# Where the tiles lie in SBUF: large tiles at multiples of 2 KB, small ones behind them

## The chip, the cores and the metric

The kernel runs on one core of a Trainium2 chip. The metric is the device time of one execution, in microseconds; each execution on the chip gives one time, and before and after are compared by the median of several.

## The reference

Two layers (`DEPTH = 2`) of a transformer block over 256 tokens of width 1024, all in float32. Per layer:

```
h = rmsnorm(x);  proj = h @ w_in                 # 1024 x 8004
aq, ak, av, bq, bk, bv, cq, ck, cv, iq, ik, iw, gl = split(proj)
y_a = differential attention(aq, ak, av)         # 4 heads, two softmaxes each
y_b = stick-breaking attention(bq, bk, bv)       # 8 heads
y_c = top-64 sparse attention(cq, ck, cv), keys picked by iq, ik, iw
merged = sum over a, b, c of sigmoid(gl) * (y @ w_br)
x = x + merged @ w_out
x = x + relu(rmsnorm(x) @ w_up)^2 @ w_down       # 1024 -> 4096 -> 1024
x = x + sigmoid(rmsnorm(x) @ w_ple_gate) * (p @ w_ple_proj)
```

## The kernel before, in words

**The products.** Every large product is made of three matmuls on numbers split in two: an operand `a` is kept as a rounded part `ah` (type float32r) and the rest `al`, and `mm3` (line 387) adds `ah*bh + ah*bl + al*bh` into one bank of PSUM. Weights come by `load_unit` (line 370): SyncE (the queue SP) starts a DMA of 256 rows x 512 columns into a tile `w`, ScalarE rounds it into `wh`, VectorE (GpSimd for a few) writes the rest to `wl`. There are 4 tiles `w`, 6 `wh` and 6 `wl`, of 4 KB in each partition.

**Two shapes.** In `chunk_T` (line 416, through `T_steps`) the weights are stationary, 128 x 128 at a time, and the activations move through the array, 256 columns, one per token. It serves `w_up`, `w_down`, `w_out`, the branch products, the gates, `bq` and `bk`, and the first layer's last products. In `chunk` (line 392) it is the other way round: the activations are stationary and 512 columns of `wh` or `wl` move (324 for the index columns, 256 where the last chunk is cut in two). It serves `q`, `k` and `v`, and the second layer's last products. The trace names the moving operand first: `mmp<-xh,wh` has `xh` moving, and `mmp<-wh,xh` has `wh` moving. Results of most products go to `mmp`, those of `w_down` to `acc`.

**The activations.** `xh` and `xl` (8 KB each, class `Norm`, line 457) hold the normalised stream that `w_in`, `w_up` and `w_ple_gate` read. For `w_ple_gate` alone they are taken from the four general slots `g8` (`spare=True`), which otherwise hold heads and gates. `yh` and `yl` (4 KB, three of each, `acts4`, line 321) hold the attention's results, the merged branches, and in the MLP the 512 hidden columns of one chunk. So in the MLP, TensorE takes turns: 96 matmuls of `up` on `xh`, `xl`, then 96 of `down` on `yh`, `yl`.

**The order of the work.** All operations are first collected by `Program`, then put in order by a list scheduler with its own costs and due times (`schedule`, line 216), and emitted at line 290, which is therefore the line of all instructions in the trace. The scheduler sees slots by pool and tag, and how many are free; it knows nothing of addresses.

**The places.** A pool takes its room in the order in which pools are opened, and its slots follow one another, each rounded up to 32 bytes. The first free byte of a partition is 16,512, which is 8 x 2048 + 128. `cp` comes first, with the identity and all constants, the residual stream `xT` among them (together 15,808 bytes); then `wp` with `w`, `wh`, `wl`; then `sp` with everything else in the order of its first use. In the program of before this gives:

```
tile                          bytes into 2048   bytes into 256
w, wh, wl, working tiles t2        1600              64
xh, xl                             1600              64
g8 (heads, gates, spare xh, xl)    1216             192
working tiles big                  1216             192
xT                                 1952             160
v (av, bv, cv)                     1024               0
yh, yl                              256               0
```

A step along the inner part of a tile (one k-tile of activations is 1024 bytes, 128 columns of weights are 512 bytes) changes the middle column and not the last.

Of the kernel before, what the change touches and what calls it, by code (L numbers as in the profile page):

```python
# [293 lines left out]
def hybrid_block(ctx: ExitStack, tc: tile.TileContext, I, out):  # L294
    nc = tc.nc
    prog = Program(nc)
    V, S, G, T, Q = (prog.engine(e) for e in ("DVE", "ACT", "POOL", "PE", "SP"))

    cp = ctx.enter_context(tc.tile_pool(name="cp", bufs=1))
    wp = ctx.enter_context(tc.tile_pool(name="wp", bufs=6))  # L300
    sp = ctx.enter_context(tc.tile_pool(name="sp", bufs=2))
    pmm = ctx.enter_context(tc.tile_pool(name="pmm", bufs=2, space=PSUM))
    ptr = ctx.enter_context(tc.tile_pool(name="ptr", bufs=2, space=PSUM))
    psc = ctx.enter_context(tc.tile_pool(name="psc", bufs=2, space=PSUM))

    def const(name, shape, dt=F32):
        return prog.tile(cp, shape, dt, name)

    def t2k(name, cols=512):
        return prog.tile(sp, [P, cols], F32, name, tag="t2", bufs=T2, ahead=AHEAD_T2)  # L310
# [2 lines left out]
        return prog.tile(sp, shape, dt, name, tag="big", bufs=5, ahead=AHEAD_BIG)  # L313

    def small(name, shape, bufs, dt=F32, tag=None):
        return prog.tile(sp, shape, dt, name, tag=tag or name, bufs=bufs)

    def g8(name, dt=F32):
        return prog.tile(sp, [P, 8, SEQ], dt, name, tag="g8", bufs=4)
# [30 lines left out]
    prog.fixed = -LEAD_LOAD + X_AFTER  # L350
    load_x(1)
    pos_i = const("pos_i", [P, NB], I32)
    Q.dma_start(out=pos_i, in_=I["positions"].rearrange("o (b p) -> p (o b)", p=P), allow_slow_non_contiguous=True)

    GAINS = ("", "idx_k_norm", "a_k_norm", "c_k_norm", "a_q_norm", "c_q_norm")
    gains = const("gains", [P, len(GAINS), DEPTH, HD])
    for i, n in enumerate(GAINS):
        if n:
# [65 lines left out]
    def rsqrt_mean(ss, n, width):  # L424

        ms = small("ms", [P, 8], 4)
        V.tensor_scalar(ms[:, :n], ss, 1.0 / width, EPS, op0=OP.mult, op1=OP.add)
        r = small("rsq", [P, 8], 10)
        G.tensor_tensor(out=r[:, :n], in0=ms[:, :n], in1=half[:, :n], op=OP.pow)
        return r[:, :n]  # L430
# [26 lines left out]
    class Norm(Acts):  # L457
# [3 lines left out]
        def __init__(self, gains, spare=False):  # L461
            if spare:
                super().__init__([(g8("xh", FR), g8("xl", FR))])
            else:
                super().__init__([tuple(small(n, [P, 8, SEQ], 1, FR) for n in ("xh", "xl"))])
            self.gains = gains
            self.ss, self.made_row = None, None
# [77 lines left out]

    first_table = S.preload_act_table_set("trig_and_small")
    ncol0, ncol = const("ncol0", [P, 8]), const("ncol", [P, 50])

    def columns(src, dst):
# [32 lines left out]
    inv = const("inv", [P, 32])  # L582
# [29 lines left out]
    identb = const("identb", [P, P], BF)  # L612
    mA = const("mA", [P, NB, NB * P], BF)
    mB = const("mB", [P, P], BF)
    negone_r, ntri_r = const("negone_r", [P, P], FR), const("ntri_r", [P, P], FR)
# [487 lines left out]
```

## Time and profile before

| | us |
|---|---|
| median of 3 runs | 998.3 (998.06 to 998.92) |
| profiled execution | 996.65 |
| its span | 994.9 |
| TensorE busy | 975.9 (98%) |
| VectorE busy | 654.1 (66%) |
| ScalarE busy | 540.6 (54%) |

A busy share says how much of the span an engine had an instruction in it. Matmuls overlap one another, so the duration of one (some 280 ns for 256 columns) is longer than the step from its start to the start of the next; the step is what a stream of them costs.

### The profile page before, as it was taken

Reading aid. Unit: us, or ns where it says so; the run is one execution under the profiler, and the core shown is the slowest. Engines: PE = TensorE matmul, PEld = TensorE weight load, DVE = VectorE, ACT = ScalarE, POOL = GpSimd, SP = SyncE. Lnnn points to the kernel's source line nnn. Section 1 sums busy time; section 2 is a strip of 40 time slices with the busy share of each in tenths; the row PEclk is TensorE's granted clock in tenths of the full one; section 3 lists DMA queues with packets and bytes.
Section 4 is the critical chain, followed back from the end, with each engine's and each line's share of the span. In section 5 each row is a group of like instructions: output and inputs, shape, how many; then the busy total and the mean of one; then the engine's idle time right before and its main releaser. Section 6 shows DMA issues by size and latency. Waiting matters only on the chain.

```text
span 994.9 us, 18435 instructions
## 1 busy us (share of the span) xinstructions
PE 975.9 (98%) x7492; PEld 922.8 (93%) x7492; DVE 654.1 (66%) x1007; ACT 540.6 (54%) x768; POOL 155.7 (16%) x137
## 2 busy tenths in 40 slices
PE   7899999999999999999999999999999999999998
PEld 6888889989999999999989888898899999999997
DVE  7748997663767455557676599975557755555573
ACT  6537674465456444456573575645745545554462
POOL 1202122314220000000312112230152100000010
PEclk9999999999999999999999999999999999999999
DMA  7564255535565656556555543556265665566551
GB/s 262 177 208 134 83 159 170 175 119 173 192 176 187 197 183 193 189 170 197 155 168 170 190 132 110 151 169 191 85 192 171 194 206 171 174 194 202 194 171 43
DMA packets 89162, 168.59 MB, mean 169 GB/s; under 512 B 5690, under 2 KB 9204, under 8 KB 89076
## 3 DMA queue, kind: packets, MB, share of 16 engines
q1 hardware_dynamic: 89076, 167.40, 53.6%
q8 instruction: 59, 0.97, 0.4%
q14 instruction: 27, 0.22, 0.1%
HBM read 166.33 MB, written 1.05 MB: 168 GB/s over the span
## 4 chain that ended last, share of the span: by engine, by line
PE 94%; DVE 3%; ACT 1%; issue 1%; DMA 1%; SPq 0%; POOL 0%; ACTq 0%; DVEq 0%
PE mmp L290 68%; PE acc L290 18%; PE z L290 2%; PE sc L290 2%; PE oc L290 1%; DVE qo L290 1%; DVE wl L290 1%; PE qps L290 1%; PE ob L290 1%; ACT wh L290 1%; PE pps L290 1%; DMA xin<-in_x 1%; DVE io L290 1%; PE xps L290 0%; DVE rm L290 0%
## 5 line engine op out<-in xcount | busy, mean ns | idle before, releaser
L290 ACT ACTIVATE wh<-w 128x1024 fp32r<-128x1024 f32 (+1 forms) x316 | 330.5, 1050 | 216.7 <-PE mmp L290 106.2
L290 DVE TENSOR_TENSOR wl<-w,wh 128x1024 fp32r<-128x1024 f32 (+1 forms) x282 | 341.8, 1220 | 154.4 <-ACT wh L290 149.1
L290 PE MATMUL mmp<-xh,wh 128*128 128x256 f32 x1088 | 310.9, 286 | 3.5 <-DVE rm L290 3.5
L290 PE MATMUL mmp<-xh,wl 128*128 128x256 f32 x1088 | 310.4, 285 | 0.0
L290 PE MATMUL mmp<-xl,wh 128*128 128x256 f32 x1088 | 309.2, 284 | 0.0
L290 PEld LDWEIGHTS mmp<-xh,wh 128*128 128x128 f32 x1088 | 208.8, 192 | 5.7 <-ACT wh L290 4.2
L290 PEld LDWEIGHTS mmp<-xh,wl 128*128 128x128 f32 x1088 | 208.6, 192 | 1.2 <-issue 1.0
L290 PEld LDWEIGHTS mmp<-xl,wh 128*128 128x128 f32 x1088 | 208.6, 192 | 0.4
L290 PE MATMUL acc<-yh,wh 128*128 128x256 f32 x512 | 141.7, 277 | 0.0
L290 PE MATMUL acc<-yl,wh 128*128 128x256 f32 x512 | 141.4, 276 | 0.0
L290 PE MATMUL acc<-yh,wl 128*128 128x256 f32 x512 | 141.4, 276 | 0.0
L290 POOL TENSOR_TENSOR wl<-w,wh 128x1024 fp32r<-128x1024 f32 x34 | 84.0, 2472 | 224.6 <-ACT wh L290 224.6
L290 PE MATMUL mmp<-wh,xh 128*128 128x512 f32 (+2 forms) x296 | 113.3, 384 | 0.3 <-ACT av L290 0.3
L290 PE MATMUL mmp<-wh,xl 128*128 128x512 f32 (+2 forms) x296 | 112.5, 381 | 0.0
L290 PE MATMUL mmp<-wl,xh 128*128 128x512 f32 (+2 forms) x296 | 111.8, 379 | 0.2 <-DVE wl L290 0.2
L290 PEld LDWEIGHTS acc<-yh,wh 128*128 128x128 f32 x512 | 96.2, 188 | 0.0
L290 PEld LDWEIGHTS acc<-yl,wh 128*128 128x128 f32 x512 | 96.2, 188 | 0.0
L290 PEld LDWEIGHTS acc<-yh,wl 128*128 128x128 f32 x512 | 96.1, 188 | 0.0
L290 PE MATMUL mmp<-yl,wh 128*128 128x256 f32 x336 | 93.1, 278 | 0.2
L290 PE MATMUL mmp<-yh,wh 128*128 128x256 f32 x336 | 93.0, 277 | 0.2 <-ACT pp L290 0.2
L290 PE MATMUL mmp<-yh,wl 128*128 128x256 f32 x336 | 92.7, 277 | 0.0
L290 POOL TENSOR_TENSOR rsq<-ms,half 128x8 f32<-128x8 f32 (+3 forms) x30 | 47.9, 1602 | 215.2 <-DVE ms L290 215.2
(194 smaller groups left out, 1198.6 us busy)
## 6 DMA issues: line engine op xcount, KB each, us to landing
w<-in_w_in SPq DMA_DIRECT2D x120, 512.0 KB, 4.0
w<-in_w_up SPq DMA_DIRECT2D x64, 512.0 KB, 3.7
w<-in_w_down SPq DMA_DIRECT2D x64, 512.0 KB, 4.7
w<-in_w_out SPq DMA_DIRECT2D x16, 512.0 KB, 4.0
w<-in_w_ple_gate SPq DMA_DIRECT2D x16, 512.0 KB, 3.8
w<-in_w_br_a SPq DMA_DIRECT2D x8, 512.0 KB, 3.7
w<-in_w_br_c SPq DMA_DIRECT2D x8, 512.0 KB, 3.7
w<-in_w_br_b SPq DMA_DIRECT2D x8, 512.0 KB, 4.2
```

The costliest lines, as they stand in the source:

```text
L290: getattr(self.engines[op.eng], op.name)(*op.args, **op.kw)
```

## The change

A third and a fourth SBUF pool (`mp`, `lp`) are opened behind `sp`, and a tile goes to a pool by its size: a multiple of 2048 bytes to `sp`, else a multiple of 256 to `mp`, else to `lp`. Of the constants only `identb`, `negone_r`, `ntri_r` and `inv` (and `ident`, which is allocated directly) stay in `cp`. Tags, numbers of slots and operations stay.

```diff
+    mp = ctx.enter_context(tc.tile_pool(name="mp", bufs=1))
+    lp = ctx.enter_context(tc.tile_pool(name="lp", bufs=1))
...
+    def pool_for(shape, dt):
+        size = math.prod(shape[1:]) * mybir.dt.size(dt)
+        return sp if size % 2048 == 0 else mp if size % 256 == 0 else lp
+
     def const(name, shape, dt=F32):
-        return prog.tile(cp, shape, dt, name)
+        first = ("identb", "negone_r", "ntri_r", "inv")
+        return prog.tile(cp if name in first else pool_for(shape, dt), shape, dt, name)
...
     def small(name, shape, bufs, dt=F32, tag=None):
-        return prog.tile(sp, shape, dt, name, tag=tag or name, bufs=bufs)
+        return prog.tile(pool_for(shape, dt), shape, dt, name, tag=tag or name, bufs=bufs)
```

## Rows read from the trace of the kernel before

**Rows 1.** The page: busy time of the engines, and the chain by engine.
```profile
PE 975.9 (98%) x7492; PEld 922.8 (93%) x7492; DVE 654.1 (66%) x1007; ACT 540.6 (54%) x768; POOL 155.7 (16%) x137
...
PE 94%; DVE 3%; ACT 1%; issue 1%; DMA 1%; SPq 0%; POOL 0%; ACTq 0%; DVEq 0%
```

**Rows 2.** The chain in order of time, MLP: start us, us, what.
```profile
360.47 10.90 PE acc L290 x96
371.37 11.50 PE mmp L290 x96
...
915.73 10.90 PE acc L290 x96
926.63 11.50 PE mmp L290 x96
```

**Rows 3.** Groups by form: TensorE, names, shape, count | busy us, mean ns.
```profile
L290 PE MATMUL mmp<-xh,wh 128*128 128x256 f32 x1088 | 310.9, 286 | 3.5 <-DVE rm L290 3.5
...
L290 PE MATMUL acc<-yh,wh 128*128 128x256 f32 x512 | 141.7, 277 | 0.0
...
L290 PE MATMUL mmp<-wh,xh 128*128 128x512 f32 x248 | 98.6, 398 | 0.0
...
L290 PE MATMUL mmp<-yh,wh 128*128 128x256 f32 x336 | 93.0, 277 | 0.2 <-ACT pp L290 0.2
...
L290 PE MATMUL mmp<-wh,xh 128*128 128x324 f32 x32 | 10.2, 319 | 0.3 <-ACT av L290 0.3
...
L290 PE MATMUL mmp<-wh,xh 128*128 128x256 f32 x16 | 4.5, 282 | 0.0
...
L290 PE MATMUL mmp<-wh,yh 128*128 128x512 f32 x8 | 3.3, 412 | 0.0
```

**Rows 4.** Timeline of TensorE, 512 columns in the first chunk: start us, us.
```profile
15.22 0.39 PE L290 MATMUL mmp<-wh,xl 128*128 128x512 f32 x1
15.44 0.39 PE L290 MATMUL mmp<-wh,xh 128*128 128x512 f32 x1
...
17.03 0.39 PE L290 MATMUL mmp<-wh,xh 128*128 128x512 f32 x1
```

**Rows 5.** Timeline of TensorE, the first layer's gate at its end.
```profile
482.73 0.28 PE L290 MATMUL mmp<-xh,wl 128*128 128x256 f32 x1
...
495.90 0.28 PE L290 MATMUL mmp<-xh,wl 128*128 128x256 f32 x1
```

**Rows 6.** Timeline of TensorE, the second layer's `w_ple_proj`.
```profile
960.23 0.39 PE L290 MATMUL mmp<-wh,yh 128*128 128x512 f32 x1
...
962.51 0.39 PE L290 MATMUL mmp<-wl,yh 128*128 128x512 f32 x1
```

**Rows 7.** Stretches: TensorE, weight loads, VectorE, ScalarE, GpSimd busy, clock, DMA.
```profile
80.00:150.00 70.00, 69.48 (x498) 60.23 (x497) 63.65 (x141) 49.58 (x86) 15.55 (x8) 1.00 0.42 126
...
301.00:470.00 169.00, 169.00 (x1452) 169.00 (x1451) 96.89 (x101) 85.93 (x102) 1.02 (x2) 1.00 0.59 188
...
570.00:640.00 70.00, 69.34 (x500) 60.11 (x498) 64.66 (x141) 49.10 (x86) 15.04 (x8) 1.00 0.43 131
```

**Rows 8.** The same stretches, TensorE's instructions that read `xh` alone.
```profile
80.00:150.00 70.00, 46.59 (x197) 1.00 0.42 126
570.00:640.00 70.00, 45.69 (x194) 1.00 0.43 131
```

**Rows 9.** The same stretches, TensorE's instructions that read `xl` alone.
```profile
80.00:150.00 70.00, 31.95 (x98) 1.00 0.42 126
570.00:640.00 70.00, 31.22 (x96) 1.00 0.43 131
```

**Rows 10.** What TensorE waited for: us in total, times, longest.
```profile
PE xps L290 <- DMA xin<-in_x: 3.5, 2, 2.1
PE mmp L290 <- DVE rm L290: 3.5, 1, 3.5
```

**Rows 11.** The page's groups: the splitting of the weights.
```profile
L290 ACT ACTIVATE wh<-w 128x1024 fp32r<-128x1024 f32 (+1 forms) x316 | 330.5, 1050 | 216.7 <-PE mmp L290 106.2
L290 DVE TENSOR_TENSOR wl<-w,wh 128x1024 fp32r<-128x1024 f32 (+1 forms) x282 | 341.8, 1220 | 154.4 <-ACT wh L290 149.1
```

**Rows 12.** Groups by form: VectorE, two adds of two SBUF operands.
```profile
L290 DVE TENSOR_TENSOR qo<-qo,rm 128x512 f32<-128x512 f32 x16 | 15.3, 956 | 0.0
L290 DVE TENSOR_TENSOR gate<-gate 128x512 f32<-128x512 f32 x16 | 11.5, 735 | 0.1
```

**Rows 13.** The page: the DMA queue's share of 16 engines.
```profile
q1 hardware_dynamic: 89076, 167.40, 53.6%
```

## The prediction

> **What bounds the kernel now.** I read the page first, for busy times and the chain; then the chain in order of time; then the groups by form, for the counts; then TensorE's timeline, for the steps from one matmul's start to the next; and last the stretches, for what stands behind TensorE. The reader is to see that TensorE is busy in 98% of the span and makes 94% of the chain that ended last [rows 1], and that it hardly waits: 3.5 us for the input at the start, 3.5 us once for VectorE, the rest shorter [rows 10]. So what counts is the step of one matmul, not its duration, for matmuls overlap.
>
> The MLP shows that step cleanly. 96 matmuls of `up` take 11.50 us and 96 of `down` take 10.90 us [rows 2], 119.8 and 113.5 ns each. Such a group of `mmp` stands 12 times in the chain, six times per layer. Both kinds have 256 columns, the same weight slots and stand in the same stretch, in which TensorE and the weight loads are busy throughout [rows 7]. They differ in the tile that moves (`xh`, `xl` against `yh`, `yl`) and in the bank written (`mmp` against `acc`). The bank isn't it: the mean duration of `mmp<-yh,wh` is 277 ns, that of `acc<-yh,wh`, and `mmp<-xh,wh` has 286 [rows 3]. What is left is the moving tile. By the table of places `yh` and `yl` begin 0 bytes past a multiple of 256, `xh` and `xl` 64 bytes past one.
>
> Two more streams test this. Where the first layer's last gate reads its `xh` from the general slots (192 past), 111 steps take 495.90 - 482.73 = 13.17 us, 118.6 ns each [rows 5]: slow too. With 512 columns of weights moving (64 past), 8 steps in the first chunk take 17.03 - 15.22 = 1.81 us, 226 ns each [rows 4]. [...] So the price of an unaligned moving operand is paid once per matmul: 119.8 - 113.5 = 6.25 ns (0.60 us over 96). [...]
>
> **The change part by part.** *The places.* `cp` keeps 512 + 128 + 256 + 512 + 512 = 1,920 bytes; 16,512 + 1,920 = 18,432 is 9 x 2048. `wp` then holds 16 slots of 4,096 bytes, and `sp` only slots that are multiples of 2,048. So `w`, `wh`, `wl`, `xh`, `xl`, `yh`, `yl`, `xT`, the heads and the working tiles all begin at a multiple of 2 KB. Nothing else changes: the scheduler counts slots by pool and tag and no tag is split over two pools, so each engine gets the same instructions in the same order, with the same waits.
>
> *Matmuls with 256 moving columns of `xh`, `xl`.* 3 x 1,088 = 3,264 [rows 3], since each such row stands for three products. At 6.25 ns they give 20.4 us.
>
> *Matmuls with weights moving.* 3 x (248 + 32 + 16 + 8) = 912 [rows 3]. No row shows them aligned. [...]
>
> *The stationary side.* It moves from 64 (or 192) to 0 as well. Where `yh` (0 past) is stationary and `wh` (64 past) moves, 10 steps take 962.51 - 960.23 = 2.28 us, 228 ns each [rows 6], no less than the 226 ns with `xh` (64 past) stationary [rows 4]. So I price it at nothing. [...]
>
> [...]
>
> *Small matmuls, transposes.* Some hundreds, mostly with `ident` moving, which stays where it is; nothing.
>
> *VectorE and ScalarE.* Their tiles move too. A 1024-element split costs 1,220 ns on VectorE and 1,050 ns on ScalarE [rows 11]; `w`, `wh` and `wl` stand at equal places within 2 KB before and after. Two adds of 512 elements from SBUF cost 735 and 956 ns [rows 12], though in each of them the operands already lie at equal places. So no row gives a price for alignment there. I take nothing; bounds are the spread of those two, 221 ns either way on each of the 32 adds, 7 us of VectorE's time in all. The cover is VectorE's idle time: 43% of the MLP, but only 6.35 of 70 us and 5.34 of 70 us in the two attention stretches [rows 7].
>
> *DMA.* The queue's packets take 53.6% of the engines' time [rows 13], and TensorE waits for a transfer only at the start [rows 10]. A faster or slower landing in aligned tiles is hidden under the queue's lead; nothing.
>
> *What is late next.* In the MLP nothing: with `up` at 10.90 us a pair takes 21.8 us, and VectorE needs 96.89 of 169 us now. In 80 to 150 and 570 to 640 us VectorE is busy 91 and 92% of the time, and 197 + 98 and 194 + 96 of the matmuls concerned run there [rows 7 to 9]: 585 x 6.25 ns = 3.7 us, which VectorE may partly take back, since its own work doesn't shrink. I count 2 us of it as lost.
>
> *The sum.* 20.4 + 5.7 - 2.0 = 24.1 us. The profiled execution took 996.65 us (span 994.9), so its counterpart is 972.5; the median of the runs is 1.65 us above it, which gives 974.2, rounded to 974.
>
> [...] The trace has the 6.25 ns between two tiles that both begin at multiples of 32 bytes [rows 2]. [...]
>
> **The rivals.** *Nothing changes.* Then `xh` is slow for another cause, such as its region of the partition: `yh`, `yl` lie above all other large tiles. Against it: the spare `xh`, `xl` in the general slots lie next below them and are slow [rows 5]. Time: 998. [...] That the change doesn't do what it says would end here too; the arithmetic of `cp` speaks against that.
>
> [...]
>
> *A collision, slower.* The slow `xh` lies at 1600 into 2 KB, as the weights do, and the fast `yh` at 256. If what costs is that the moving and the stationary read start at the same place within 2 KB, then `xh` gains nothing and the 2,544 matmuls on `yh`, `yl` now pay 6.25 ns: 15.9 us, 1014. Against it: `xh` at 1216 is slow against weights at 1600 [rows 5], and `wh` at 1600 is slow against `yh` at 256 [rows 6]. It decides from 0.8 ns per matmul on `yh`, where 2 us are lost and nothing is won.
>
> *Half of it.* Only the 256-column matmuls gain and VectorE takes back all 3.7 us: 20.4 - 3.7 = 16.7 us, 982.
>
> **How the numbers follow.** About 0.2%, 2 us, is what runs of this kernel can tell from no change. Forecast 0.70 (from 968, the weights' full bound, to 980), half of it 0.08, both sides 0.10, nothing 0.07, collision 0.05. The range from 953 to 984 leaves out the last two and the deeper half of "both sides". Faster 0.88, same 0.07, slower 0.05.
>
> **What would show it.** Right: the groups of 96 on `mmp` in the MLP at 10.9 us, as those on `acc`, which stay; 512-column steps at 220 ns instead of 226; the mean of `mmp<-xh,wh` near 277 ns; VectorE's share above 92% in the first attention stretch. Wrong: `up` still at 11.50 us; `acc` groups over 10.90 us (collision) or under 10.7 us (both sides); changed durations of the splitting on VectorE or ScalarE; a new wait of TensorE on `wl` or `qo` of more than 2 us in total.

## The result and the profile after

The changed kernel is slower: 1012.31 us (1010.8 to 1012.6) against 998.61 us in the same runs, ratio 1.0139, 95% interval 1.0127 to 1.0152. The forecast was 974, the range ended at 984. The profiled execution took 1010.8 us, its span is 1009.1 us, 14.2 more than before.

The page after: busy times, then the chain by engine.

```profile
PE 990.4 (98%) x7492; PEld 937.1 (93%) x7492; DVE 652.9 (65%) x1007; ACT 540.5 (54%) x768; POOL 156.0 (15%) x137
...
PE 94%; DVE 3%; ACT 1%; DMA 1%; SPq 0%; issue 0%; POOL 0%; ACTq 0%; DVEq 0%
```

Against [rows 1] the numbers of instructions are the same, and so are VectorE, ScalarE and GpSimd to within 1.2 us. TensorE alone is busy longer, by 14.5 us. The chain after, in order of time (start us, us, what), shows where:

```profile
362.83 11.52 PE acc L290 x96
374.35 11.52 PE mmp L290 x96
...
928.30 11.52 PE acc L290 x96
939.82 11.52 PE mmp L290 x96
```

The groups of `up` on `xh` stayed (11.50 before, 11.52 now), and the groups of `down` on `yh` rose from 10.90 to 11.52 us [rows 2]: 120.0 ns per matmul for all. The groups by form (count | busy us, mean ns of one) say the same of all matmuls with 256 columns that read `yh`, in the MLP and in the branches, and that 512 columns kept their duration:

```profile
L290 PE MATMUL mmp<-xh,wh 128*128 128x256 f32 x1088 | 310.5, 285 | 3.5 <-DVE rm L290 3.5
...
L290 PE MATMUL acc<-yh,wh 128*128 128x256 f32 x512 | 145.1, 283 | 0.0
...
L290 PE MATMUL mmp<-wh,xh 128*128 128x512 f32 x248 | 98.3, 397 | 0.0
...
L290 PE MATMUL mmp<-yh,wh 128*128 128x256 f32 x336 | 95.0, 283 | 0.0
```

In [rows 3] these are 286, 277, 398 and 277. So nothing got faster, and the 3 x (512 + 336) = 2,544 matmuls on `yh`, `yl` got slower. Eight groups of `down` in each of two layers, 16 x 0.62 us, are 9.9 us. The branch products and `w_out` lie between the attention and the MLP. The chain before and after, first layer, from the last long piece of attention to the first group of `acc`:

```profile
227.24 37.27 PE mmp L290 x323
...
315.67 10.90 PE acc L290 x96
```

```profile
226.11 72.99 PE mmp L290 x605
...
316.75 11.52 PE acc L290 x96
```

Before, this took 315.67 - 227.24 = 88.43 us, after 90.64: 2.2 us more, and 3.0 us more in the second layer, read in the same way. The changed kernel came to this point 1.1 us earlier. 9.9 + 5.2 - 1.1 = 14.0 of the 14.2 us. The 1.1 us need not come from the change: the profiled execution before ran from 22 to 42 us at a granted clock of 0.91, the one after at 1.00.

### The profile page after: what moved, and what is told of

It reads as the page before. It is cut to its first block, busy times and chain, and to the rows that moved or that the text cites. A ratio compares the mean times of both kernels' runs of the same rounds, so it can differ in the third digit from the quotient of the medians.

```text
span 1009.1 us, 18435 instructions
## 1 busy us (share of the span) xinstructions
PE 990.4 (98%) x7492; PEld 937.1 (93%) x7492; DVE 652.9 (65%) x1007; ACT 540.5 (54%) x768; POOL 156.0 (15%) x137
## 4 chain that ended last, share of the span: by engine, by line
PE 94%; DVE 3%; ACT 1%; DMA 1%; SPq 0%; issue 0%; POOL 0%; ACTq 0%; DVEq 0%
PE mmp L290 68%; PE acc L290 18%; PE z L290 2%; PE sc L290 2%; PE oc L290 1%; DVE qo L290 1%; PE qps L290 1%; DMA w<-in_w_in 1%; PE ob L290 1%; DVE wl L290 1%; PE pps L290 1%; DVE io L290 1%; ACT wh L290 0%; SPq L290 0%; DVE rm L290 0%
## 5 line engine op out<-in xcount | busy, mean ns | idle before, releaser
L290 PE MATMUL acc<-yh,wh 128*128 128x256 f32 x512 | 145.1, 283 | 0.0
L290 PE MATMUL acc<-yh,wl 128*128 128x256 f32 x512 | 144.9, 283 | 0.0
L290 PE MATMUL acc<-yl,wh 128*128 128x256 f32 x512 | 144.9, 283 | 0.0
L290 PEld LDWEIGHTS acc<-yl,wh 128*128 128x128 f32 x512 | 98.3, 192 | 0.0
L290 PEld LDWEIGHTS acc<-yh,wh 128*128 128x128 f32 x512 | 98.3, 192 | 0.0
L290 PEld LDWEIGHTS acc<-yh,wl 128*128 128x128 f32 x512 | 98.3, 192 | 0.0
```

The lines of the kernel that those rows point to most:

```text
L290: getattr(self.engines[op.eng], op.name)(*op.args, **op.kw)
```

## The experiments

The prediction put the slow step down to a moving operand off a multiple of 256 bytes. After the change all are on one, and all are slow. What is left: the moving and the stationary operand get in each other's way, or collide, when they start at certain places relative to each other (the rival that was forecast at 1014); or only some places are good for the moving operand itself (256 past 2 KB); or the region of the partition counts. Below, "difference" is the weights' place less the moving operand's, within 256 bytes. Room for padding comes from a reserved region at the bottom of the partition that is made 2 KB smaller (8 KB in the survey); `y_plus256`, which has this too, takes as long as the changed kernel.

**y_as_weights.** The kernel before; only `yh`, `yl` move.

```diff
+    yp = ctx.enter_context(tc.tile_pool(name="yp", bufs=1))      # behind sp
+    yp.tile([P, 456], F32, name="before_y")
...
-        return tuple(prog.tile(sp, [P, 4, SEQ], FR, n, tag=n, bufs=3) for n in ("yh", "yl"))
+        return tuple(prog.tile(yp, [P, 4, SEQ], FR, n, tag=n, bufs=3) for n in ("yh", "yl"))
```

> The kernel before with yh, yl alone moved from 256 to 1600 bytes past a multiple of 2 KB, the place of the weights; they stay the highest large tiles of the partition. Collision theory: acc groups of 96 go from 10.90 to 11.50 us, the time to about 1012 to 1014. Alignment theory of the prediction (a moving operand off a multiple of 256 costs 6.25 ns): the same, 1014. Region theory (high addresses are good): nothing moves, 998.

Measured: 1012.45 us, ratio 1.0140 (1.0125 to 1.0155). Its chain:

```profile
364.23 11.52 PE acc L290 x96
375.75 11.52 PE mmp L290 x96
```

Moving these six tiles and, within 2 KB, no other large one costs all that the change costs. They stay the highest large tiles, so the region theory falls. Collision and alignment are both still possible.

**y_plus256.** The changed kernel, `yh`, `yl` in a pool of their own behind 256 bytes of padding (`before_y` of 64 floats).

> The changed kernel with the six tiles yh, yl moved to 256 bytes past a multiple of 2 KB, where they stood before; weights and xh, xl at multiples of 2 KB. Theory of the moving operand's own place (256 past 2 KB is good): acc groups of 96 return to 10.90 us, mmp groups on xh stay at 11.50, and the time returns to about 998. Collision theory with places compared within 2 KB: the same, 998. Collision theory with places compared within 256 bytes or less: nothing moves, 1012. Region theory: 1012.

Measured: 1012.44 us, ratio 1.0139 (1.0124 to 1.0154), all groups of 96 at 11.52 us. The old place of `yh` by itself is not what was good: own place falls, and a collision must compare places within 256 bytes or less.

**w_plus64.** The changed kernel, weights moved.

```diff
+    cp.tile([P, 16], F32, name="before_w")
+    wq.tile([P, 496], F32, name="after_w")      # a pool between wp and sp
```

The few small constants in `cp`, such as `ident`, move by the same 64 bytes.

> The changed kernel with w, wh, wl moved as a block to 64 bytes past a multiple of 2 KB; every other large tile stays at a multiple of 2 KB (room is made by a smaller reserved region at the bottom of the partition, 2 KB less). Collision theory (a moving operand costs 6.25 ns more where it starts at the same place as the stationary one): now xh, xl, yh, yl all differ from the weights as yh did before, so the MLP groups of 96 fall to 10.9 us on mmp as well as on acc, and 6,720 matmuls x 6.3 ns give about 42 us under the changed kernel's 1012: some 970 to 980. Theory of the moving operand's own place (256 past 2 KB is good, 0 is bad): nothing moves, 1012, all groups of 96 at 11.50 us. Theory of the region of the partition: nothing moves, 1012.

Measured: 984.65 us, ratio 0.9861 (0.9844 to 0.9877). All activations are where the changed kernel has them within 2 KB; of the large tiles the weights alone moved, and `xh` is fast as well. Its chain, a pair in the first and a pair in the second layer:

```profile
360.74 11.31 PE acc L290 x96
372.04 11.31 PE mmp L290 x96
...
846.75 10.88 PE acc L290 x96
857.63 10.88 PE mmp L290 x96
```

That is the collision theory's forecast for the groups of the second layer, though the time misses its 970 to 980. And there is one thing that it didn't say: at the same difference a stream runs at 10.88 us or at 11.31, 113.3 or 117.8 ns per matmul, and keeps to one for nearly all of a layer's MLP (the first layer's last group changes to the lower one).

**xy_plus192.** The same difference, made from the other side: weights at 0, and 192 bytes of padding (`after_w` of 48 floats, no `before_w`) ahead of the pool with all activations.

> The changed kernel with weights at multiples of 2 KB and xh, xl, yh, yl (with the rest of their pool) 192 bytes past one: the difference of w_plus64, made by moving the other side. If only the difference within 256 bytes counts: as w_plus64, 984 to 992, MLP groups of 96 at 10.9 or 11.3 us. If the weights' own place at 64 past is what is good: as the changed kernel, 1012.

Measured: 983.74 us (981.5 to 992.94), ratio 0.9876 (0.9842 to 0.9910). In its profile both layers run at the lower step:

```profile
356.01 10.88 PE acc L290 x96
366.89 10.88 PE mmp L290 x96
...
859.73 10.88 PE acc L290 x96
870.61 10.88 PE mmp L290 x96
```

Here the constants stay. So at this difference it doesn't matter which side is moved: neither side's own place explains the gain. This version and `w_plus64` beat both kernels. The time stays above 970 to 980 although every group of 96 in the chain is at the lower step or within 0.02 us of it, for outside the MLP the step is higher: the branch products and gates before it take 118.3 ns each.

```profile
224.94 44.24 PE mmp L290 x374
```

**survey32.** All rows of `xh`, `xl`, `yh`, `yl`, `wh`, `wl` padded by 32 bytes, so that differences vary from matmul to matmul (`padded_shape=[P, 4, SEQ + 8]`, `[P, 8, SEQ + 8]`, `[P, 2, 520]`).

> The changed kernel with 32 bytes of padding behind each 256-column row of xh, xl, yh, yl and behind each 512-column row of wh, wl, so that moving and stationary operands meet at all differences that are multiples of 32 bytes. Collision theory: the step of a 256-column matmul depends on the difference of the two starts within 256 bytes and not on either alone: about 120 ns at difference 0, 113.5 where the moving one lies 192 past or 64 short, others in between. Own-place theory: it depends on the moving start alone. Region theory: 120 ns for all. Time: between 975 and 1012 by the first, by which share of pairs collides.

Measured: 1005.09 us, one execution. Its chain:

```profile
386.20 11.31 PE acc L290 x96
397.52 11.42 PE mmp L290 x96
```

Nowhere 10.88, nowhere 11.52. Groups mix the differences, so nothing could be read for a single difference. The next kernels hold it constant instead.

**w_plus32 to w_plus224.** As `w_plus64`, with other sizes of the two pads.

> As w_plus64, with the weights 32 bytes past a multiple of 2 KB. Grain of 64 bytes or more (the two reads collide while they start in the same 64 bytes): nothing gained against the changed kernel, 1012, MLP groups of 96 at 11.50 us. Finer grain: between 985 and 1012, groups between 10.9 and 11.5 us.

> As w_plus64, with the weights 96 bytes past. Grain of 64 bytes: as w_plus64, 985, groups of 96 at 10.9 or 11.3 us. Finer grain, with the distance deciding: some other value, below 985 if w_plus64 is still half in collision.

> As w_plus64, with the weights 128 bytes past. In the kernel before, the first layer's last gate meets the weights at this difference and has 118.6 ns per matmul: by places compared within 256 bytes, 6,720 matmuls x 1.3 ns under the changed kernel, about 1003. By places compared within 128 bytes: as the changed kernel, 1012, all groups at 11.50 us.

> As w_plus64, with the weights 160 bytes past: fills the map in steps of 32 bytes. Between w_plus128 (1010) and w_plus192 (1005) if the cost goes smoothly with the difference; no theory here says more.

> As w_plus64, with the weights 192 bytes past, so that the moving operand stands 64 past the weights within 256 bytes instead of 64 short. If only the size of the difference counts: as w_plus64, 985. If the sign counts (the weights must lie ahead of the moving operand): between 1000 and 1012.

> As w_plus64, with the weights 224 bytes past. By symmetry with w_plus32: 1007. If the side counts that lies ahead: as w_plus192, 1005, or up to the changed kernel's 1012.

Measured: 1006.82, 1011.24, 1009.67, 1017.08, 1004.83 and 1003.80 us. One row of each one's chain, in this order, from the first layer's MLP:

```profile
340.98 11.36 PE acc L290 x96
```

```profile
340.12 11.52 PE acc L290 x96
```

```profile
342.41 11.39 PE acc L290 x96
```

```profile
343.88 11.52 PE acc L290 x96
```

```profile
340.01 11.31 PE acc L290 x96
```

```profile
339.03 11.31 PE acc L290 x96
```

| difference, bytes | kernel | ns per 256-column matmul in the MLP | ratio to before (interval) |
|---|---|---|---|
| 0 | changed | 120.0 | 1.0139 (1.0127 to 1.0152) |
| 32 | w_plus32 | 118.3 | 1.0084 (1.0068 to 1.0100) |
| 64 | w_plus64 | 113.3 or 117.8 | 0.9861 (0.9844 to 0.9877) |
| 96 | w_plus96 | 120.0 | 1.0128 (1.0112 to 1.0145) |
| 128 | w_plus128 | 118.6 | 1.0108 (1.0089 to 1.0128) |
| 160 | w_plus160 | 120.0 | 1.0196 (1.0176 to 1.0216) |
| 192 | w_plus192 | 117.8 | 1.0061 (1.0044 to 1.0079) |
| 224 | w_plus224 | 117.8 | 1.0063 (1.0043 to 1.0083) |

The third column is the group's time over 96, from the one profiled execution of each kernel. The theory that two reads are free unless they start in the same 64 bytes falls with `w_plus96`, symmetry with `w_plus192` (1004.83 us against 984.65), and a smooth course with `w_plus160`. Only at 64 do the MLP's groups reach 113.3 ns. `w_plus128` has the 118.6 ns that the first layer's last gate had before [rows 5], at the same difference and with tiles at other places; its time, 1009.67, missed the 1003 that was worked out from this.

The third column isn't a fixed price of a difference. In `w_plus192` the same tiles, `xh` moving against the weights, also run at the lower step: this stretch of the second layer's first products takes 11.33 us for 100 steps, 113.3 ns each, where its MLP has 117.8.

```profile
538.99 0.28 PE L290 MATMUL mmp<-xl,wh 128*128 128x256 f32 x1
...
550.32 0.28 PE L290 MATMUL mmp<-xh,wl 128*128 128x256 f32 x1
```

`w_plus160` is slower than the changed kernel though its groups of 96 are the same. Its row for 512 columns, where weights move and `xh` is stationary:

```profile
L290 PE MATMUL mmp<-wh,xh 128*128 128x512 f32 x248 | 99.7, 403 | 0.0
```

6 ns more than after the change, and there are 744 such matmuls: 4.5 us, if each step grew as its duration did, where the kernel is 4.8 us slower. That isn't the whole account. `w_plus96` has 402 ns in this row and the same groups of 96, and is no slower than the changed kernel. Outside its MLP the step is lower: its branch products and gates take 117.9 ns each, those of `w_plus160` 120.7 (first layers of `w_plus96` and `w_plus160`).

```profile
227.97 44.08 PE mmp L290 x374
```

```profile
230.17 73.00 PE mmp L290 x605
```

With 512 columns no difference beat equal places: the means are 397 to 399 ns in the four kernels where `xh` stands at 0 from the weights, 399 and 400 at 64, and 401 to 403 at the others.

**Not the other engines, nor DMA.** ScalarE and VectorE read and write the weight slots too, and DMAs fill the tiles ahead of them, so a collision with these had to be excluded. The changed kernel's MLP has stretches in which VectorE and ScalarE stand still, and others in which no DMA runs (TensorE, weight loads, VectorE, ScalarE, GpSimd busy, clock, DMA share, GB/s):

```profile
330.60:334.00 3.40, 3.40 (x31) 3.40 (x30) 0.00 (x0) 0.00 (x0) 0.00 (x0) 1.00 0.84 257
358.00:361.00 3.00, 3.00 (x28) 3.00 (x27) 1.48 (x2) 2.96 (x4) 0.00 (x0) 1.00 0.00 0
```

TensorE's timeline in the first and in the second (start us, us):

```profile
330.63 0.28 PE L290 MATMUL mmp<-xh,wh 128*128 128x256 f32 x1
...
333.99 0.28 PE L290 MATMUL mmp<-xl,wh 128*128 128x256 f32 x1
```

```profile
357.75 0.28 PE L290 MATMUL mmp<-xl,wh 128*128 128x256 f32 x1
...
360.99 0.28 PE L290 MATMUL mmp<-xl,wh 128*128 128x256 f32 x1
```

28 steps in 3.36 us and 27 in 3.24 us: 120 ns in both. The same matmuls are slow without the one and without the other, which leaves two parties that are TensorE's own: its reads of the moving operand and of the weights that it loads meanwhile. That they collide is argued and not shown: no run took the weight loads away, and no stretch of the changed kernel's MLPs had the other engines and DMA still at once for even one step. What is shown is that the places of the two operands relative to each other change the step.

## Why the prediction was wrong

**What bounds the kernel** was right: TensorE's step is what counts, and nearly the whole difference lies there. So was the reading that the tile read and not the bank written makes the MLP's two steps differ.

**The step that failed** is the cause given for it: "So the price of an unaligned moving operand is paid once per matmul". That it is paid once per matmul was the author's estimate from two steps, 119.8 ns for 256 columns and 226 ns for 512 [rows 2, rows 4]; no run shows what the columns alone take. `xh` was slow because it stood at the place of the weights within 256 bytes, not because it stood 64 past a multiple; `yh` was fast because the weights stood 64 past it. In the trace before, both explanations fit the MLP, since there is one place for `xh` and the weights and another for `yh`. The change took away that distance: the `down` groups went from 10.90 to 11.52 us, while `up` stayed slow. Moving the weights by 64 bytes brought `up` on an unmoved `xh` to 10.88 and 11.31 us.

**The terms.** 20.4 us for `xh`, `xl`: measured nothing, 11.50 to 11.52 us per group. 5.7 us for moving weights: nothing, 398 to 397 ns. No run shows the 6.25 ns per matmul behind these 5.7 us (912 matmuls), nor the full bound of the weights behind 968, nor a gain from both sides such as the lower end, 953, allows for: with both sides aligned the 512-column mean went from 398 to 397 ns and no group of 96 fell. `yh` and `yl`, for which the sum has no term: a loss of 15.1 us (9.9 + 5.2), where the collision rival had 15.9. VectorE's and ScalarE's own work and DMA: nothing, as forecast. The 2.0 us counted off for VectorE were not put to the test, since nothing got faster.

**The rivals.** The collision, given 0.05, forecast 1014; 1012 came, and its sign, `acc` groups over 10.90 us. Its own condition, equal places within 2 KB, was too narrow: `y_plus256` is slow with its tiles 256 bytes from that. Both rows held against it were misread, for they refute only a collision at equal places and at nothing else. The gate with `xh` in the general slots stands at a difference of 128, and 128 costs 118.6 ns [rows 5], as `w_plus128` shows. The 512-column matmuls against `yh` [rows 6] are slow at every difference held constant (412 to 417 ns for `mmp<-wh,yh`). "Both sides", given 0.10, was the opposite of the truth: with both aligned, all groups of 96 take 11.52 us. "Nothing changes" fell too: the changed kernel takes 1012.31 us against 998.61, and 64 bytes count, 984.65 us in `w_plus64`.

With the same instructions, 0.62 us per 96 matmuls hang on where the two operands start: 10.90 us before, 11.52 us after.

**Open.** What two reads would share, why the MLP reaches the lower step at 64 bytes and not at 192, and what picks one of two steps at 64 and at 192. `w_plus64` had executions of 984.02 to 985.24 us and one of 992.09, the profiled one, with its first layer at 11.31 us; `xy_plus192` had 981.5 to 984.61 and one of 992.94. The 13 groups of that layer in the chain, at 11.31 instead of 10.88, are 5.6 of the some 7.4 us between the profiled execution and the median.

## What to carry to other kernels

Where TensorE is the bound, the place of the moving operand relative to the stationary one is a parameter to be tuned: with float32r, 256 moving columns and 128 stationary ones, it was worth up to 6% of the step here (113.3 against 120.0 ns), and round addresses, the same for both, were among the worst (120.0 ns). When two explanations fit all rows because the kernel has only two layouts, move one tile alone (a pad of some bytes) before the whole layout is rebuilt. And a counterexample refutes only the form of a theory that it meets: "not at equal places" is not "no collision".

## What was not expected of the hardware

The step of a stream of matmuls at a fixed layout is not one number: at a difference of 64 bytes, TensorE kept to 113.3 or to 117.8 ns per matmul through nearly a whole MLP, in one execution both, one per layer; at 192 bytes, one execution had 113.3 in the second layer's first products and 117.8 in its MLP. And what helps 256 columns did not help 512: the step of 256 columns fell from 120.0 to 113.3 ns at a difference of 64, while the mean duration of 512 columns was 397 to 399 ns at equal places, 399 and 400 ns at 64 and 401 to 403 ns at the others.
